# One-hot look-ups of a top-k selection: fp32 on VectorE and GpSimd, or bf16 on VectorE alone

## The chip, the cores and the metric

The kernel runs on one core of a Trainium2 chip. The core has five instruction streams: PE (TensorE, matrix products; its weight loads are listed apart as PEld), DVE (VectorE), ACT (ScalarE), POOL (GpSimd) and SP (SyncE, which here issues most DMA transfers). Each runs its own instructions in order and waits on semaphores for the others. Tiles lie in SBUF, results of PE in PSUM banks. The metric is device microseconds (us) of one execution.

## The reference

One step of a hybrid layer for 128 sample tokens (8 sequences of 16) and 256 prompt tokens: an RWKV-7 branch and a sparse-attention branch, mixed and added to x, then a PEER layer (a mixture over 16384 single-neuron experts), `x = x + gate2 * PEER(h2)`. The change lies in PEER's choice of experts. For each token and each of 8 heads a query of 128 numbers is cut into two halves. Each half is scored against 128 keys, and the 16 best keys of each half are kept, with their scores and indices. Their 256 sums are candidates, of which the 16 best are kept. Position p in the sorted candidates belongs to position p1 in the first list and p2 in the second; the expert is `i1[p1] * 128 + i2[p2]`. The look-ups are the two steps i1[p1] and i2[p2]: for each token, head and half, 16 positions (0 to 15) are replaced by the key indices (0 to 127) that stand there. The 16 sums go through a softmax to give the experts' weights; the layer's output is the sum over the experts of weight times gelu(h2 . u_e) times v_e.

## The kernel before

Tokens lie on the 128 partitions, in three groups: i = 0 is the sample group, i = 1 and 2 are the prompt. The branches and the mixing take the time up to about 840 us. Then come the query products and scores, the selection, and the experts. For the prompt all 16384 experts are computed densely, in 128 blocks of 128 (`dense_u` for h2 . u with a gelu, `weights` for the matrix of weights per token and expert, `dense_v` for the products with v). For the sample group the chosen experts' rows are gathered (`peer_sparse`): per pick, POOL issues an indirect DMA (line 1518), DVE multiplies the row of u by h2 and sums (line 1529), ACT takes the gelu of four such sums (line 1532, tile `dots`), and DVE adds dots times the row of v into `acc` (line 1539). Heads are gathered in two halves, so `peer_select` is called four times: for i = 0 with four heads, twice, then for i = 1 and i = 2 with eight heads. The gathers run on beside everything that follows.

In `peer_select` (lines 1255 to 1341) DVE finds each list's 16 best by max, max_index and match_replace (lines 1273 to 1277), casts the indices to fp32 (`sif`, line 1279, tag `psf`), POOL adds the candidates (line 1284), DVE finds the best 16 of them (lines 1293 to 1297), and from their places in the candidate list works out the positions in the two sorted lists (`jf`, tag `pjf`, lines 1299 to 1309, with `st`, tag `pst`, as an aid). The look-ups follow, in blocks of one half and four heads, so 2 + 2 + 4 + 4 = 12 blocks. A block is a tile of 128 partitions x 4 heads x 16 picks x 16 places: DVE compares each pick's position with 0 to 15 (line 1315, a one-hot), POOL multiplies by the key indices (line 1317), DVE sums over the 16 places (line 1318). The tile's tag `poh` has two buffers, so the third block can begin only when the sum of the first is done; the same tag held a transposed h2 before.

Behind the look-ups come the softmax (Exp on ACT, line 1322), and for i = 0 the row numbers for the gathers, for i = 1 and 2 three transposes whose result `weights` needs.

The order of the instructions on each engine isn't written by hand: the tile framework orders them by a simulated timeline, so that the selection is interleaved with `dense_u`, the gathers and the beginning of `weights`. Tags and their numbers of buffers set who must wait for whom. The fp32 weights of most dense blocks are cut into a high and a low part (line 227 on ACT, line 231 on DVE or POOL), and some 36 blocks are multiplied whole. `G` (line 1445, ACT) is the gelu that empties the PSUM bank of a `dense_u` block (tag `fx`).

Of the kernel before, what the change touches and what calls it, by code (L numbers as in the profile page):

```python
# [14 lines left out]
BF16 = mybir.dt.bfloat16  # L15
I32 = mybir.dt.int32
U32 = mybir.dt.uint32
AF = mybir.ActivationFunctionType
OP = mybir.AluOpType
AX = mybir.AxisListType  # L20
# [172 lines left out]
class K:  # L193
# [1034 lines left out]
    def scores_head(self):  # L1228
        nc = self.nc
        self.h2f = self.t([128, 8, 256], tag="h2f", pool=self.qpool)  # L1230
        self.keysT = self.t([128, 8, 128], tag="keysT", pool=self.qpool)
        nc.sync.dma_start(self.keysT, self.I["keysT"])
        self.qp = self.t([128, 8, NT], tag="qp", pool=self.qpool)

    def scores_s(self, u):

        nc = self.nc
        W = self.wload(self.I["w_pq"][:, u], 256)
        q = self.t([128, 256], tag="pq")
        nc.scalar.activation(q, self.natp(W, 256, self.h2T, 0), AF.Copy)  # L1240
        p = self.ps([128, 2, 128], tag="cp")
        for c in range(2):
            nc.tensor.transpose(p[:, c], q[:, c * 128:(c + 1) * 128], self.ident)
        nc.scalar.activation(self.qp[:, 2 * u:2 * u + 2, 0:128], p, AF.Copy)
# [10 lines left out]
    def peer_select(self, i, h0=0, nh=8):  # L1255

        nc = self.nc
# [4 lines left out]
        for hb in range(0, nh, 4):  # L1262
            for half in range(2):
                pr = slice(64 * half, 64 * half + 64)
                p = self.ps([128, 4, 128], tag="dx")
# [4 lines left out]
                for c in range(4):  # L1270
                    h = hb + c
# [6 lines left out]
        sif = self.t([128, 2, 8, 16], tag="psf")[:, :, :nh]  # L1278
# [21 lines left out]
        jf = self.t([128, 2, 8, 16], tag="pjf")[:, :, :nh]  # L1300
# [7 lines left out]
        nc.vector.scalar_tensor_tensor(st, j1, 64.0, st, op0=OP.add, op1=OP.min)  # L1308
        nc.vector.tensor_tensor(j2, j2, st, op=OP.subtract)
        idx = self.t([128, 2, 8, 16], tag="pix", bufs=2)[:, :, :nh]  # L1310
        for half in range(2):
            for h in range(0, nh, 4):
                hs = slice(h, h + 4)
                oh = self.t([128, 4, 16, 16], tag="poh", bufs=2)
                nc.vector.tensor_tensor(oh, jf[:, half, hs].unsqueeze(3).to_broadcast([128, 4, 16, 16]),
                                        self.c["io16"].unsqueeze(1).unsqueeze(1).to_broadcast([128, 4, 16, 16]), op=OP.is_equal)
                nc.gpsimd.tensor_tensor(oh, oh, sif[:, half, hs].unsqueeze(2).to_broadcast([128, 4, 16, 16]), op=OP.mult)
                nc.vector.tensor_reduce(out=idx[:, half, hs], in_=oh, op=OP.add, axis=AX.X)

        gw = self.t([128, nh, 16], tag=f"pg{i}{h0}", pool=self.pool if i else self.hpool2)  # L1320
        nc.vector.tensor_tensor(gw, fv, fv[:, :, 0:1].to_broadcast([128, nh, 16]), op=OP.subtract)
# [13 lines left out]
        p = self.ps([128, 3, 128], tag="dx")  # L1335
# [362 lines left out]
```

## Time and profile before

| | us |
|---|---|
| runs | 1856.91, 1863.67, 1869.19 (median 1863.67) |
| profiled execution | 1860.99, span 1859.2 |
| look-ups, first start to last | 917.1 to 1097.8 |
| busy, PE / DVE / ACT / POOL | 1740.9 / 1379.4 / 693.3 / 724.1 |

A row of a line reads: line, engine, operation, result <- inputs by tile names, how many, then least/median/longest ns. In rows that group a stretch, "x" counts instructions and the figures stand in microseconds. "DMA share" is the mean busy share of the 16 DMA engines; PEclk is the granted clock of TensorE, 1.00 being full. A wait is written as who waited (engine, tile, line) <- for whom, with its total, its number and its longest.

### The profile page before, as it was taken

How to read it: one execution, taken by the hardware profiler on the slowest of the kernel's cores; microseconds unless marked ns; L12 is line 12 of the kernel's file. 1: busy time of each engine (PE TensorE's matmuls, PEld its weight loads, DVE VectorE, ACT ScalarE, POOL GpSimd, SP SyncE). 2: the span in 40 equal slices, each digit the busy share in tenths (PEclk: the TensorE clock that was granted, in tenths of full speed). 3: DMA queues.
4: the chain of work that ended last, by engine and by line, in shares of the span. 5: the costliest groups of instructions: out<-in, count | busy, mean ns of one | idle time of the engine just before them, and what ended most of it. 6: DMA issues, size and time to landing. Idle time of an engine off the chain costs nothing. (4 is left out here: it accounts for less than half of the span.)

```text
span 1859.2 us, 33617 instructions
## 1 busy us (share of the span) xinstructions
PE 1740.9 (94%) x12621; PEld 1436.3 (77%) x12621; DVE 1379.4 (74%) x2905; ACT 693.3 (37%) x1402; POOL 724.1 (39%) x763
## 2 busy tenths in 40 slices
PE   7997999999999989899988979999999888999998
PEld 4985888877877867798877869999975556776765
DVE  4549678767767745445999999899967777787773
ACT  4432333333243333334221135478842222333332
POOL 2331333223223210024255566563346676465541
PEclk8996999999999989899998989999999999999999
DMA  8421563454264274655487969975489999999994
GB/s 307 141 79 34 168 224 91 147 168 137 78 218 137 70 243 151 213 174 179 148 313 284 359 244 331 383 291 182 164 294 369 375 374 356 351 373 344 347 344 157
DMA packets 181083, 434.11 MB, mean 233 GB/s; under 512 B 39348, under 2 KB 78388, under 8 KB 180920
## 3 DMA queue, kind: packets, MB, share of 16 engines
q1 hardware_dynamic: 144056, 297.73, 46.8%
q0 software_dynamic: 36864, 134.23, 19.3%
q8 instruction: 99, 1.62, 0.3%
q14 instruction: 64, 0.52, 0.1%
HBM read 401.65 MB, written 30.24 MB: 232 GB/s over the span
## 5 line engine op out<-in xcount | busy, mean ns | idle before, releaser
L231 DVE TENSOR_TENSOR wl<-w,wh 128x1024 fp32r<-128x1024 f32 x278 | 351.2, 1269 | 138.5 <-PE mm L223 64.3
L227 ACT ACTIVATE wh<-w 128x1024 fp32r<-128x1024 f32 x282 | 295.3, 1053 | 221.6 <-PE mm L223 88.0
L223 PE MATMUL fx<-h2h,wl 128*128 128x256 f32 x736 | 214.3, 291 | 10.4 <-DVE wl L231 10.3
L1518 POOL DMA_INDIRECT raw<-in_pu,pe x128 | 161.9, 1265 | 154.5 <-DVE acc L1539 46.6
L223 PE MATMUL fx<-h2h,wh 128*128 128x256 f32 x736 | 215.6, 293 | 4.3 <-ACT wh L227 3.2
L1518 POOL DMA_INDIRECT raw<-in_pv,pe x128 | 169.8, 1327 | 121.0 <-PE dx L223 45.4
L223 PE MATMUL fx<-h2l,wh 128*128 128x256 f32 x736 | 209.8, 285 | 0.0
L1539 DVE SCALAR_TENSOR_TENSOR acc<-raw,dots,acc 128x1024 f32<-128x1024 f32 x127 | 169.8, 1337 | 17.9 <-DMA raw<-in_pv,pe 16.7
L1529 DVE SCALAR_TENSOR_TENSOR raw<-raw,sh 128x1024 f32<-128x1024 f32 x128 | 163.4, 1291 | 17.1 <-DMA raw<-in_pu,pe 16.7
L223 PEld LDWEIGHTS fx<-h2h,wl 128*128 128x128 f32 x736 | 140.1, 190 | 14.4 <-DVE wl L231 12.7
L223 PEld LDWEIGHTS fx<-h2h,wh 128*128 128x128 f32 x736 | 140.9, 191 | 10.1 <-ACT wh L227 4.5
L223 PE MATMUL fx<-h2f,w 128*128 128x256 f32 x576 | 133.5, 394 | 14.4 <-ACT G L1445 14.4
L223 PEld LDWEIGHTS fx<-h2l,wh 128*128 128x128 f32 x736 | 140.4, 191 | 2.1 <-issue 1.7
L223 PEld LDWEIGHTS fx<-h2f,w 128*128 128x128 f32 x576 | 112.9, 198 | 33.3 <-ACT G L1445 16.4
L223 PE MATMUL mm<-LTh,wh 128*128 128x384 f32 (+1 forms) x344 | 121.9, 355 | 1.7 <-ACT wh L227 1.0
L223 PE MATMUL mm<-LTl,wh 128*128 128x384 f32 (+1 forms) x344 | 120.7, 351 | 1.2 <-POOL LTl L477 1.2
L223 PE MATMUL mm<-LTh,wl 128*128 128x384 f32 (+1 forms) x344 | 121.0, 352 | 0.0
L223 PE MATMUL mm<-wh,LTh 128*128 128x256 f32 (+1 forms) x360 | 105.4, 293 | 0.6 <-ACT qx L876 0.6
L223 PE MATMUL mm<-wh,LTl 128*128 128x256 f32 (+1 forms) x360 | 104.6, 291 | 0.0
L223 PE MATMUL mm<-wl,LTh 128*128 128x256 f32 (+1 forms) x360 | 104.4, 290 | 0.0
L1367 POOL TENSOR_TENSOR G<-G,wg 128x144 f32<-128x144 f32 (+1 forms) x64 | 61.7, 988 | 85.6 <-ACT wg L1364 85.5
L223 PEld LDWEIGHTS mm<-wh,LTh 128*128 128x128 f32 x360 | 70.1, 195 | 4.6 <-issue 2.7
(549 smaller groups left out, 4193.3 us busy)
## 6 DMA issues: line engine op xcount, KB each, us to landing
w<-in_puT SPq DMA_DIRECT2D x128, 512.0 KB, 6.1
w<-in_pv SPq DMA_DIRECT2D x128, 512.0 KB, 6.8
w<-in_w_in SPq DMA_DIRECT2D x70, 512.0 KB, 4.5
w<-in_w_ada SPq DMA_DIRECT2D x48, 512.0 KB, 4.2
cKT<-in_cKT SPq DMA_DIRECT2D x32, 256.0 KB, 4.2
cV<-in_cV SPq DMA_DIRECT2D x32, 256.0 KB, 4.5
w<-in_w_pq SPq DMA_DIRECT2D x16, 512.0 KB, 3.6
d<-wst SPq DMA_DIRECT2D x8, 832.0 KB, 4.3
```

The lines of the kernel that those rows point to most:

```text
L223: return self.nc.tensor.matmul(out, l, r, start=start, stop=stop, skip_group_check=True, **kw)
L227: self.nc.scalar.activation(hi, src, AF.Copy)
L231: (self.nc.vector if eng == "v" else self.nc.gpsimd).tensor_tensor(lo, src, hi, op=OP.subtract)
L1367: (nc.vector if w is p else nc.gpsimd).tensor_tensor(g, g, w[:, :, c0:c1], op=OP.mult)
L1518: d = nc.gpsimd.indirect_dma_start(out=u, out_offset=None, in_=src, in_offset=bass.IndirectOffsetOnAxis(ap=e[:, j:j + 1], axis=0))
L1529: nc.vector.scalar_tensor_tensor(u, u, 1.0, h2, op0=OP.mult, op1=OP.mult, accum_out=dots[:, j:j + 1])
L1539: nc.vector.scalar_tensor_tensor(acc, v, dots[:, j:j + 1], acc, op0=OP.mult, op1=OP.add)
```

## The change

A constant `ioe` is made once: the numbers 0 to 15 in bf16, each repeated 16 times, so that its inner dimension runs over 16 equal values. In each call the positions are copied to bf16 (`jb`). A block's tile `o2` holds two bf16 halves in the same number of bytes as the fp32 tile before: the one-hot and the spread indices. ACT copies the key indices into the second half, spread over the picks. DVE compares `jb` with `ioe`; the order of the dimensions is now head, place, pick, so that picks are innermost. DVE multiplies the halves, in bf16, and sums over the places, which now lie 16 elements (32 bytes) apart. All numbers are whole and below 256, which bf16 holds exactly. POOL's twelve multiplications are gone.

```diff
@@ scores_head
         self.qp = self.t([128, 8, NT], tag="qp", pool=self.qpool)
+        self.ioe = self.t([128, 16, 16], BF16, tag="ioe", pool=self.qpool)
+        nc.vector.tensor_copy(self.ioe, self.c["io16"].unsqueeze(2).to_broadcast([128, 16, 16]))
@@ peer_select
         idx = self.t([128, 2, 8, 16], tag="pix", bufs=2)[:, :, :nh]
+        jb = self.t([128, 2, 8, 16], BF16, tag="pjb")[:, :, :nh]
+        nc.vector.tensor_copy(jb, jf)
         for half in range(2):
             for h in range(0, nh, 4):
                 hs = slice(h, h + 4)
-                oh = self.t([128, 4, 16, 16], tag="poh", bufs=2)
-                nc.vector.tensor_tensor(oh, jf[:, half, hs].unsqueeze(3).to_broadcast([128, 4, 16, 16]),
-                                        self.c["io16"].unsqueeze(1).unsqueeze(1).to_broadcast([128, 4, 16, 16]), op=OP.is_equal)
-                nc.gpsimd.tensor_tensor(oh, oh, sif[:, half, hs].unsqueeze(2).to_broadcast([128, 4, 16, 16]), op=OP.mult)
-                nc.vector.tensor_reduce(out=idx[:, half, hs], in_=oh, op=OP.add, axis=AX.X)
+                o2 = self.t([128, 2, 4, 16, 16], BF16, tag="poh", bufs=2)
+                nc.scalar.activation(o2[:, 1], sif[:, half, hs].unsqueeze(3).to_broadcast([128, 4, 16, 16]), AF.Copy)
+                oh, sx = o2[:, 0], o2[:, 1]
+                nc.vector.tensor_tensor(oh, jb[:, half, hs].unsqueeze(2).to_broadcast([128, 4, 16, 16]),
+                                        self.ioe.unsqueeze(1).to_broadcast([128, 4, 16, 16]), op=OP.is_equal)
+                nc.vector.tensor_tensor(oh, oh, sx, op=OP.mult)
+                nc.vector.tensor_reduce(out=idx[:, half, hs], in_=oh.rearrange("p h c k -> p h k c"), op=OP.add, axis=AX.X)
```

In the kernel after, line 1319 is the copy on ACT, 1321 the comparison, 1323 the multiplication, 1324 the sum, 1314 the copy of the positions; other lines of `peer_select` up to there stand 2 further down, lines behind it 6.

The order on the engines moves with the edit. First DVE, at the first two blocks of i = 1 (`pjf` and `pjb` are the positions, `pix` the result, `acc` and `raw` the gathered experts). Before:

```order
L1306 TENSOR_SCALAR pst_11001<-pjf_10997 128x128
L1315 TENSOR_TENSOR poh_11007<-pjf_10997,clate 128x1024
L1315 TENSOR_TENSOR poh_11011<-pjf_10997,clate 128x1024
L1539 SCALAR_TENSOR_TENSOR acc_11650<-raw_12293,dots_12147,acc_11650 128x1024
L1307 SCALAR_TENSOR_TENSOR pst_11001<-pjf_10997,pst_11001 128x128
L1539 SCALAR_TENSOR_TENSOR acc_11650<-raw_12360,dots_12147,acc_11650 128x1024
L1318 TENSOR_REDUCE pix_11006<-poh_11007 128x64
L1308 SCALAR_TENSOR_TENSOR pst_11001<-pjf_10997,pst_11001 128x128
L1539 SCALAR_TENSOR_TENSOR acc_11650<-raw_12363,dots_12147,acc_11650 128x1024
L1318 TENSOR_REDUCE pix_11006<-poh_11011 128x64
```

After, at the same blocks:

```order
L1314 CAST pjb_11017<-pjf_11007 128x256
L1539 TENSOR_TENSOR dots_12169<-dots_12169,pg_2022_10501 128x4
L1321 TENSOR_TENSOR poh_11019<-pjb_11017,ioe_9835 128x1024
L1321 TENSOR_TENSOR poh_11024<-pjb_11017,ioe_9835 128x1024
L1545 SCALAR_TENSOR_TENSOR acc_11672<-raw_12312,dots_12169,acc_11672 128x1024
L1323 TENSOR_TENSOR poh_11019<-poh_11019 128x1024
L1323 TENSOR_TENSOR poh_11024<-poh_11024 128x1024
L1545 SCALAR_TENSOR_TENSOR acc_11672<-raw_12315,dots_12169,acc_11672 128x1024
L1324 TENSOR_REDUCE pix_11016<-poh_11019 128x64
L1324 TENSOR_REDUCE pix_11016<-poh_11024 128x64
```

The two multiplications stand on DVE now, between comparison and sum, and the arithmetic on `pst` is all done before the first comparison, since `jb` is copied for both halves at once.

On POOL, at the first blocks of i = 0 (`pcd` are the candidates). Before:

```order
L1284 TENSOR_TENSOR pcd_10658<-psv_10592 128x4x56
L1284 TENSOR_TENSOR pcd_10658<-psv_10592 128x4x8
L1317 TENSOR_TENSOR poh_10487<-poh_10487,psf_10444 128x1024
L1284 TENSOR_TENSOR pcd_10658<-psv_10592 128x4x16
L1317 TENSOR_TENSOR poh_10491<-poh_10491,psf_10444 128x1024
L1518 DMA raw_11652<-in_pu,pe_2023_10504 128x1024
```

After:

```order
L1286 TENSOR_TENSOR pcd_10664<-psv_10598 128x4x56
L1286 TENSOR_TENSOR pcd_10664<-psv_10598 128x4x8
L1286 TENSOR_TENSOR pcd_10664<-psv_10598 128x4x16
L1524 DMA raw_11674<-in_pu,pe_2025_10510 128x1024
L1524 DMA raw_11677<-in_pu,pe_2025_10510 128x1024
```

The multiplications are gone, and the candidates and the gathers follow one another.

On ACT, at the third and fourth block of i = 1. Before:

```order
L1445 ACTIVATE G_11261<-fx_11434 128x256
L1445 ACTIVATE G_11261<-fx_11446 128x256
L1445 ACTIVATE G_11261<-fx_11458 128x256
L1445 ACTIVATE G_11261<-fx_11470 128x256
L1269 ACTIVATE psc_11043<-dx_11038 128x512
```

After:

```order
L1538 ACTIVATE dots_12169<-dots_12169 128x4
L1451 ACTIVATE G_11283<-fx_11468 128x256
L1319 ACTIVATE poh_11029<-psf_10950 128x1024
L1451 ACTIVATE G_11283<-fx_11480 128x256
L1319 ACTIVATE poh_11034<-psf_10950 128x1024
L1451 ACTIVATE G_11283<-fx_11492 128x256
```

The copies of the spread indices stand between the gelus of the dense experts; each of these two waits for the sum of the block whose buffer it takes.

## The prediction

> **What bounds the kernel now.** I read the page first, for the span and for which engine is fullest over the whole.
>
> ```profile
> span 1859.2 us, 33617 instructions
> PE 1740.9 (94%) x12621; PEld 1436.3 (77%) x12621; DVE 1379.4 (74%) x2905; ACT 693.3 (37%) x1402; POOL 724.1 (39%) x763
> ```
>
> PE is busy 94% of the span, so the look-ups can shorten the kernel only where PE stands idle. The edited lines run between 917 and 1098 us (the rows of the look-ups below give their first and last start), so the second view is the table of stretches, cut at those times and at the changes of work behind them.
>
> ```profile
> core 0: us, PE busy (x) PEld busy (x) DVE busy (x) ACT busy (x) POOL busy (x), PEclk, DMA share, GB/s
> 917.00:1100.00 183.00, 156.71 (x716) 132.84 (x714) 182.42 (x587) 35.47 (x73) 100.98 (x78) 0.93 0.79 286
> 1100.00:1400.00 300.00, 294.19 (x2294) 280.12 (x2295) 267.88 (x372) 192.34 (x419) 148.75 (x125) 1.00 0.76 277
> 1400.00:1600.00 200.00, 177.20 (x625) 117.26 (x624) 152.74 (x192) 52.60 (x83) 126.03 (x105) 0.95 0.99 371
> 1600.00:1859.20 259.20, 247.83 (x1131) 182.83 (x1129) 183.72 (x224) 88.77 (x135) 117.46 (x90) 0.99 0.86 316
> ```
>
> In the stretch of the selection DVE is busy 182.42 of 183.00 us, and PE only 156.71: 26.3 us of PE time are lost here, more than in any other of these rows but the DMA-bound one and nearly as much as there (22.8 and 11.4 us in the last two, 5.8 us in the second). DVE sets the pace of the selection, and an average of 74% hides it. Behind it, from 1100 to 1400 us, PE is busy 98%; from 1400 to 1600 us the DMA engines are at 0.99.
>
> The third view is the waits in that stretch (who waited for whom, total, times, longest).
>
> ```profile
> ACT G L1445 <- PE fx L223: 65.4, 21, 6.2
> ACT dots L1532 <- DVE raw L1529: 42.8, 7, 10.0
> PE fx L223 <- ACT G L1445: 14.4, 5, 5.7
> POOL poh L1317 <- DVE poh L1315: 8.6, 5, 4.5
> ```
>
> The chain is DVE first: ACT waits 42.8 us for the gathered dot products (line 1529) before their gelu (line 1532); the gelus of the dense experts (G, line 1445) queue behind that on ACT; and PE waits 14.4 us for those to free its PSUM banks. So whatever DVE saves here should be felt by PE, and what holds ACT is felt by PE too.
>
> **The change part by part.** These are the rows of the look-ups (least/median/longest ns of one, then first and last start).
>
> ```profile
> L1315 DVE TENSOR_TENSOR poh<-pjf,clate x12: 1206/1214/1270, 917.1 to 1085.5; 128x1024 f32<-128x1024 f32 x12
> L1317 POOL TENSOR_TENSOR poh<-poh,psf x12: 2352/3189/3349, 918.4 to 1088.8; 128x1024 f32<-128x1024 f32 x12
> L1318 DVE TENSOR_REDUCE pix<-poh x12: 1193/1207/1216, 923.0 to 1097.8; 128x64 f32<-128x1024 f32 x12
> L1307 DVE SCALAR_TENSOR_TENSOR pst<-pjf,pst x4: 2124/2312/2434, 918.6 to 1073.6; 128x64 f32<-128x64 f32 x2, 128x128 f32<-128x128 f32 x2
> L1308 DVE SCALAR_TENSOR_TENSOR pst<-pjf,pst x4: 197/240/281, 921.3 to 1079.3; 128x64 f32<-128x64 f32 x2, 128x128 f32<-128x128 f32 x2
> ```
>
> Lines 1307 and 1308 do the same operation on the same shapes, and one takes 2312 ns where the other takes 240. The timeline (start, duration) shows why; after the first pair stand the six other long DVE instructions of the stretch, and the usual durations of their lines in it.
>
> ```profile
> 918.39 2.35 POOL L1317 TENSOR_TENSOR poh<-poh,psf 128x1024 f32<-128x1024 f32 x1 [4.48 <-DVE poh L1315]
> 918.62 2.19 DVE L1307 SCALAR_TENSOR_TENSOR pst<-pjf,pst 128x64 f32<-128x64 f32 x1
> ...
> 960.78 2.85 DVE L1529 SCALAR_TENSOR_TENSOR raw<-raw,sh 128x1024 f32<-128x1024 f32 x1
> 995.32 3.37 DVE L1539 SCALAR_TENSOR_TENSOR acc<-raw,dots,acc 128x1024 f32<-128x1024 f32 x1
> 1009.50 3.36 DVE L1529 SCALAR_TENSOR_TENSOR raw<-raw,sh 128x1024 f32<-128x1024 f32 x1
> 1075.99 3.37 DVE L1529 SCALAR_TENSOR_TENSOR raw<-raw,sh 128x1024 f32<-128x1024 f32 x1
> 1086.59 3.36 DVE L231 TENSOR_TENSOR wl<-w,wh 128x1024 fp32r<-128x1024 f32 x1
> 1089.87 3.39 DVE L1539 SCALAR_TENSOR_TENSOR acc<-raw,dots,acc 128x1024 f32<-128x1024 f32 x1
> ```
>
> ```profile
> L1529 DVE SCALAR_TENSOR_TENSOR raw<-raw,sh x28: 1186/1208/3372, 940.8 to 1082.0; 128x1024 f32<-128x1024 f32 x28
> L1539 DVE SCALAR_TENSOR_TENSOR acc<-raw,dots,acc x26: 1258/1271/3393, 953.3 to 1098.9; 128x1024 f32<-128x1024 f32 x26
> L231 DVE TENSOR_TENSOR wl<-w,wh x3: 1209/1215/3362, 1086.6 to 1096.6; 128x1024 fp32r<-128x1024 f32 x3
> ```
>
> The POOL multiplication that starts at 918.39 ends at 920.74, and the DVE instruction that starts beside it ends at 920.81: a DVE instruction with two inputs in SBUF stands until POOL's is done. The "busy" of DVE contains this standing. *Removed: the hold-ups.* Line 1307: 4 x (2.31 - 0.24) = 8.3 us. The six others: 19.70 us in sum, less 3 x 1.208 + 2 x 1.271 + 1.215 = 7.38, gives 12.3. Together -20.6 us of DVE. I take it whole, because no POOL operation of that kind takes the place of the 12; the gathers' POOL instructions stay as they were, and the three additions for the candidates (line 1284) too.
>
> For the rest these rows give prices; the last three are of the view that groups by line and shape (us in all, then mean ns of one).
>
> ```profile
> L1354 DVE TENSOR_TENSOR oh<-wA,wB x64: 670/683/1142, 1115.3 to 1357.8; 128x512 f32<-128x512 f32 x64
> L1279 DVE CAST psf<-psi x4: 203/258/367, 904.0 to 1053.4; 128x128 f32<-128x128 uint32 x2, 128x256 f32<-128x256 uint32 x2
> L1301 DVE CAST pjf<-pja x4: 214/410/1625, 915.0 to 1068.7; 128x128 f32<-128x128 uint32 x2, 128x256 f32<-128x256 uint32 x2
> L227 ACT ACTIVATE wh<-w x5: 1043/1043/1057, 1083.6 to 1094.2; 128x1024 fp32r<-128x1024 f32 x5
> ```
>
> ```profile
> L684 DVE TENSOR_TENSOR TX<-TL,NL 48x225 f32<-48x225 f32 x8 | 4.8, 604 | 0.1
> L687 DVE COPY TX<-TL 48x256 f32<-48x256 f32 x8 | 3.2, 406 | 0.2
> L686 DVE TENSOR_REDUCE TL<-TX 48x15 f32<-48x225 f32 x8 | 3.0, 376 | 0.2
> ```
>
> *Comparison, now bf16.* Same 1024 columns, half the bytes. No row of before has a two-input instruction with only bf16; the bounds are the fp32 row, 1.214 us (no gain), and the time of half as many fp32 elements, 0.683 us (line 1354). I take the lower, because both operands now run along 16 adjacent elements of two bytes: 12 x (0.683 - 1.214) = -6.4 us (to 0). [...]
>
> *Multiplication, moved to DVE.* 12 more instructions, +8.2 us at 0.683 (to +14.6 at 1.214).
>
> *Reduction, now over a stride.* It sums bf16 elements 32 bytes apart. Its time now is 1.207 us for 1024 elements; with the 0.376 us of the 225-element reduction (line 686) that is (1207 - 376) / 799 = 1.04 ns per element and 0.142 us fixed. Line 687 reads one input transposed, with a step of 16 words: on that line 256 elements would take 0.408 us, and it takes 0.406, so no surcharge. Line 684 reads two inputs with such a step: 604 ns, where 225 elements on that line take 376, so 1.01 ns per element more. The change has one strided input; the nearest row is 687, whose surcharge is nil, and I take a little above it, +2 us for the 12. The bounds are 0 and 12 x 1024 x 1.01 ns = +12.4 us.
>
> *The bf16 copy of the positions* (line 1314 of after): 4 casts of 128 or 256 columns by line 1279, 4 x 0.26 = +1.1 us; line 1301 was once held to 1.6 us, so up to +6.5. The constant `ioe` is one more such cast, +0.3 us, in the mixing stage where PE is the busy one; there it costs nothing, and 0.3 us without that cover.
>
> *Spread indices, on ACT.* 12 copies of 128x1024 by line 227, 12 x 1.043 = 12.5 us, on an engine busy 35.47 of 183 us. Their input is ready with the cast of line 1279, long before the positions; but eight of the twelve also need a `poh` buffer, which the reduction of two blocks earlier frees. While ACT stands there, its queue behind it (qp, the score copies, G) stands, and PE for their banks; and DVE's multiplication needs the copy. Bounds: 0, and the 14.4 us that PE stands behind ACT today a second time; I take +2 us.
>
> The sum on DVE: -20.6 - 6.4 + 8.2 + 2 + 1.1 + 2 = -13.7 us. What is late next is PE, with 26.3 - 13.7 = 12.6 us of idle left, so the stretch can shrink by that much. From 1100 to 1400 us PE is 98% busy and its work only starts sooner, so the gain passes through. For the part behind it, 200 of 759 us are at a DMA share of 0.99; I take that quarter of the gain as lost and keep three quarters, -10 us. Against the profiled execution's own 1860.99 us (1.8 us around the span) that is 1851; the median of the runs, 1863.67, stands 2.7 us above that execution.
>
> **The rivals.**
>
> *The strided reduction pays.* For it: line 684. Against it: line 687. Price: halfway, since one of two inputs is strided, 12 x 1024 x 0.5 ns = +6.2 in place of +2, so -9.5 on DVE and -7 at the end: 1854. At the whole surcharge -3.3, so -2.5 at the end: 1858. [...]
>
> *Everything carries.* No surcharge, no ACT wait, no loss behind: -20.6 - 6.4 + 8.2 + 1.1 = -17.7, so 1843. For it: DVE's 99.7%, PE's idle of 26.3 us. Against it: the DMA share of 0.99.
>
> *The gain is swallowed.* PE reaches the DMA-bound stretch earlier and waits there: 1861. For it: 0.99 and 371 GB/s. Against it: the share is 0.76 and 0.79 before, so transfers have room to move forward.
>
> *ACT's queue blocks (slower).* Each of the eight copies that need a freed buffer stands for as long as PE's waits behind ACT last today, 14.4 / 5 = 2.9 us, and DVE and PE stand with it: 8 x 2.9 = 23 us in place of my 2, against -15.7 for the rest, +7; with the three quarters for what gains and losses carry, 1866, and at the longest such wait, 8 x 5.7 = 46, up to 1884. It decides from a mean wait of 15.7 / 8 = 2.0 us. For it: ACT executes in order, and DVE's backlog makes it wait up to 10.0 us today. Against it: the copies are small beside 81% idle time.
>
> *bf16 brings nothing (slower, or the change doesn't do what it says).* Both two-input instructions at 1.214 and the whole stride: -20.6 + 14.6 + 12.4 + 1.1 + 2 = +9.5, so 1868. [...] Against it: the adjacent inner runs.
>
> **How the numbers follow.** Forecast 1851: 0.33. Strided reduction 1854 to 1858: 0.20. Everything carries, 1843: 0.18. Swallowed, 1861: 0.12. ACT blocks, 1866 to 1884: 0.10. bf16 brings nothing, 1868: 0.07. The range from 1837 to 1872 takes in all of these but the worse half of the ACT case, and at the low end leaves some 6 us, about the distance between two runs of before, for the order of the other work, which changes with the edit. A measurement can tell 1% of 1863.67, 18.6 us: faster means below 1845, slower above 1882. Faster: most of "everything carries" and the lower edge of the forecast, 0.25. Slower: the tail of the ACT case and some of the unpriced reordering, 0.07. Within 1%: 0.68.
>
> **What would show it.** Right: no DVE instruction of 2 us or more in the look-ups; line 1307 (1309 of after) at 0.24 us; comparison and multiplication near 0.68, reduction near 1.2; POOL busy some 38 us less in the stretch (12 x 3.189); the selection's end earlier by 10 to 15 us with DVE still above 95%. Wrong: the reduction at 1.7 us or more; comparison at 1.2; ACT waiting for the reduction (line 1324 of after) by 2 us or more at a time; or the selection shorter and the stretch with the DMA at 0.99 longer by the same.

## The result and the profile after

| kernel | median us | runs | ratio to before (95%) |
|---|---|---|---|
| before | 1861.96 | 11 | |
| after | 1851.03 | 11 | 0.9942 (0.9920 to 0.9965) |

The change makes the kernel 10.9 us faster, 0.6%, and the interval excludes no change. The profiled execution of after has a span of 1850.2 us. Its look-ups, from the view of single lines (least/median/longest ns, first and last start):

```profile
L1309 DVE SCALAR_TENSOR_TENSOR pst<-pjf,pst x4: 200/278/293, 920.1 to 1069.8; 128x64 f32<-128x64 f32 x2, 128x128 f32<-128x128 f32 x2
L1314 DVE CAST pjb<-pjf x4: 219/284/357, 923.0 to 1070.8; 128x128 bf16<-128x128 f32 x2, 128x256 bf16<-128x256 f32 x2
L1319 ACT ACTIVATE poh<-psf x12: 1039/1056/1057, 906.9 to 1079.8; 128x1024 bf16<-128x1024 f32 x12
L1321 DVE TENSOR_TENSOR poh<-pjb,ioe x12: 680/688/754, 924.2 to 1082.5; 128x1024 bf16<-128x1024 bf16 x12
L1323 DVE TENSOR_TENSOR poh<-poh x12: 683/686/751, 927.4 to 1083.8; 128x1024 bf16<-128x1024 bf16 x12
L1324 DVE TENSOR_REDUCE pix<-poh x12: 1982/2002/2134, 930.2 to 1088.7; 128x64 f32<-128x1024 bf16 x12
```

The 2.3 us of line 1307 (here 1309) have become 0.28; comparison and product take 0.69 each; and the sum over the 32-byte step takes 2.00 us where 1.21 stood. From the table of stretches, the selection counted from the first cast of the key indices (line 1279, here 1281) to the end of the last sum. Before:

```profile
core 0: us, PE busy (x) PEld busy (x) DVE busy (x) ACT busy (x) POOL busy (x), PEclk, DMA share, GB/s
904.00:1099.00 195.00, 169.27 (x776) 143.11 (x774) 194.42 (x685) 36.65 (x75) 101.91 (x80) 0.93 0.76 275
```

After:

```profile
906.70:1090.70 184.00, 165.58 (x776) 141.63 (x774) 182.19 (x698) 44.78 (x84) 73.45 (x67) 0.96 0.81 289
```

The selection is 11.0 us shorter, with DVE still busy 99%; 776 products of PE lie in either. POOL's busy time has fallen by 28 us and not by the 38 that the prediction names as a sign: its 12 products had taken 34.7 us in all (2.91 us in the mean, where 12 times the median was reckoned), and its other work in the stretch took 6 us more. ACT's has risen by 8. One instruction of DVE that isn't part of the look-ups still stands, a gathered dot product of 2.22 us beside an addition of candidates on POOL (line 1286). What follows takes as long as before: from the start of the selection's last act, the copy of the second transposed result on ACT (line 1339, after 1345), to the end of the span.

```profile
L1339 ACT ACTIVATE pT<-dx x2: 491/491/491, 1021.0 to 1099.5; 128x384 f32<-128x384 f32 x2
```

```profile
L1345 ACT ACTIVATE pT<-dx x2: 490/490/490, 1014.2 to 1091.3; 128x384 f32<-128x384 f32 x2
```

1859.2 - 1099.5 = 759.7 us before, 1850.2 - 1091.3 = 758.9 after. This difference is called "the rest" below. Single executions reach the selection at different times: its first cast starts between 903.5 and 913.3 us in the profiles of this document, and line 1023, some 750 us earlier, already between 152.0 and 160.5. The start of the last `pT` moves with that. So the experiments are read by the rest and by the length of the selection, from its first cast to the last `pT`: 195.5 us before and 184.6 after.

### The profile page after: what moved, and what is told of

Its sections match the earlier page's. It is cut to its first block, busy times and chain, and to the rows that moved or that the text cites. A ratio compares the mean times of both kernels' runs of the same rounds, so it can differ in the third digit from the quotient of the medians.

```text
span 1850.2 us, 33639 instructions
## 1 busy us (share of the span) xinstructions
PE 1736.5 (94%) x12621; PEld 1434.4 (78%) x12621; DVE 1372.4 (74%) x2922; ACT 702.0 (38%) x1412; POOL 684.7 (37%) x751
## 5 line engine op out<-in xcount | busy, mean ns | idle before, releaser
L1524 POOL DMA_INDIRECT raw<-in_pu,pe x128 | 163.1, 1274 | 178.3 <-DVE acc L1545 42.5
L1373 POOL TENSOR_TENSOR G<-G,wg 128x144 f32<-128x144 f32 (+1 forms) x64 | 55.7, 894 | 88.7 <-ACT wg L1370 88.7
L223 PEld LDWEIGHTS mm<-LTh,wh 128*128 128x128 f32 (+1 forms) x344 | 66.6, 194 | 10.1 <-issue 3.6
```

The source lines that it names most:

```text
L223: return self.nc.tensor.matmul(out, l, r, start=start, stop=stop, skip_group_check=True, **kw)
L1373: (nc.vector if w is p else nc.gpsimd).tensor_tensor(g, g, w[:, :, c0:c1], op=OP.mult)
L1524: d = nc.gpsimd.indirect_dma_start(out=u, out_offset=None, in_=src, in_offset=bass.IndirectOffsetOnAxis(ap=e[:, j:j + 1], axis=0))
```

## The experiments

The theory: DVE's time in the selection sets when the selection ends, and that moment goes to the end of the kernel one to one; the change took the hold-ups by POOL away and gave a good part of it back in the strided sum. The rivals: a quarter or all of a gain is lost in the DMA-bound stretch; the hold-ups cost nothing at the end; ACT's queue takes a part. All medians, ratios to before with 95% intervals, and from each profile the starts of the first cast and of the last `pT`, the time between them, and the rest. Each ratio is taken against executions of before that were run beside that kernel, with medians from 1860.66 to 1863.29 us, so a difference of medians of two rows holds up to 2.6 us of that:

| kernel | median us | ratio | first cast | last pT | selection | rest |
|---|---|---|---|---|---|---|
| before | 1861.96 | | 904.0 | 1099.5 | 195.5 | 759.7 |
| after | 1851.03 | 0.9942 (0.9920 to 0.9965) | 906.7 | 1091.3 | 184.6 | 758.9 |
| e1_tree | 1843.18 | 0.9899 (0.9871 to 0.9927) | 908.6 | 1081.4 | 172.8 | 762.9 |
| e2_fp32_dve | 1872.78 | 1.0063 (1.0042 to 1.0084) | 903.5 | 1106.0 | 202.5 | 763.6 |
| g_fp32 | 1860.27 | 0.9985 (0.9969 to 1.0002) | 911.3 | 1102.6 | 191.3 | 759.7 |
| e3_twice | 1896.34 | 1.0179 (1.0148 to 1.0211) | 913.3 | 1136.3 | 223.0 | 759.4 |
| g_twice | 1881.68 | 1.0119 (1.0090 to 1.0148) | 909.3 | 1123.8 | 214.5 | 755.4 |
| e4_bf16_pool | 1857.11 | 0.9981 (0.9958 to 1.0004) | 906.8 | 1095.8 | 189.0 | 756.4 |
| e6_bufs4 | 1857.14 | 0.9967 (0.9944 to 0.9990) | 908.0 | 1093.4 | 185.4 | 762.7 |
| t_gate40 | 1846.83 | 0.9915 (0.9884 to 0.9946) | 910.8 | 1066.4 | 155.6 | 777.7 |
| t_wide | 1843.05 | 0.9913 (0.9883 to 0.9942) | 905.5 | 1070.5 | 165.0 | 767.1 |

### e1_tree: no strided sum

```diff
-                nc.vector.tensor_reduce(out=idx[:, half, hs], in_=oh.rearrange("p h c k -> p h k c"), op=OP.add, axis=AX.X)
+                for m in (8, 4, 2):
+                    nc.vector.tensor_tensor(oh[:, :, :m], oh[:, :, :m], oh[:, :, m:2 * m], op=OP.add)
+                nc.vector.tensor_tensor(idx[:, half, hs], oh[:, :, 0], oh[:, :, 1], op=OP.add)
```

> Kernel after, with the strided reduction (12 x 2.002 us) replaced by four bf16 additions that halve the places (512, 256, 128 and 64 results), all over adjacent picks. By the 0.688 us of a bf16 product of 1024 columns and the 0.25 us of small two-input instructions the four take about 0.42 + 0.28 + 0.22 + 0.24 = 1.16 us, so DVE gets back 12 x 0.84 = 10 us. Theory 'DVE's time in the selection goes to the end one to one': 1841 us. Rival 'a quarter is lost in the DMA-bound stretch': 1843.5. Rival 'DVE's time there does not end the kernel, the gain came from POOL's relief or from the order': 1851.

Measured 1843.18 us. The additions, by line:

```profile
L1325 DVE TENSOR_TENSOR poh<-poh x36: 210/280/475, 932.2 to 1076.9; 128x512 bf16<-128x512 bf16 x12, 128x256 bf16<-128x256 bf16 x12, 128x128 bf16<-128x128 bf16 x12
L1326 DVE TENSOR_TENSOR pix<-poh x12: 201/217/230, 937.0 to 1078.3; 128x64 f32<-128x64 bf16 x12
```

Their durations come to 11.1 + 2.6 us for the 12 blocks, 1.14 us per block in place of 2.00. The ends of short instructions overlap with what follows; counted from each start to DVE's next start it is 0.81 us per block, where the strided sum has 1.92. The selection is 11.8 us shorter than in after, and the median falls by 7.9. So DVE's time in the selection does carry to the end; between one to one (1841) and three quarters (1843.5) this run doesn't decide. Part of it stops at PE: DVE ends its last sum 12.3 us earlier than in after (at 1078.5 and 1090.8 us), but the transposes of that sum then stand behind other products in PE's queue, and the last `pT` starts 9.9 us earlier. e1_tree is clearly faster than before; against after the two intervals overlap.

### e2_fp32_dve and g_fp32: the hold-ups alone

The kernel before, with one word changed:

```diff
-                nc.gpsimd.tensor_tensor(oh, oh, sif[:, half, hs].unsqueeze(2).to_broadcast([128, 4, 16, 16]), op=OP.mult)
+                nc.vector.tensor_tensor(oh, oh, sif[:, half, hs].unsqueeze(2).to_broadcast([128, 4, 16, 16]), op=OP.mult)
```

> Kernel before, with the fp32 multiplication on VectorE in place of GpSimd and nothing else. Theory 'the hold-ups of DVE by POOL cost 20.6 us': -20.6 + 12 x 1.214 = -6 us, 1856 if all of it carries, 1857.5 at three quarters; no DVE instruction with two inputs over 2 us is left. Rival 'the hold-ups hid behind something': +14.6 us, 1876. Rival 'bf16 alone made the gain': slower than before by some us.

Measured 1872.78 us, 11.5 us slower than before on the same chip, not 6 faster. As far as the time goes, the theory failed here. The hold-ups are gone in the profile all the same:

```profile
L1307 DVE SCALAR_TENSOR_TENSOR pst<-pjf,pst x4: 204/249/291, 918.2 to 1085.0; 128x64 f32<-128x64 f32 x2, 128x128 f32<-128x128 f32 x2
L1317 DVE TENSOR_TENSOR poh<-poh,psf x12: 1205/1220/1226, 918.3 to 1099.4; 128x1024 f32<-128x1024 f32 x12
```

So something else was added. The view that groups DVE's lines, from the selection's first cast to the last `pT`, shows it (count, busy us, mean ns, idle time before and what ended it). Before:

```profile
L1529 DVE SCALAR_TENSOR_TENSOR raw<-raw,sh 128x1024 f32<-128x1024 f32 x28 | 40.1, 1434 | 0.0
L1539 DVE SCALAR_TENSOR_TENSOR acc<-raw,dots,acc 128x1024 f32<-128x1024 f32 x26 | 37.5, 1442 | 0.3 <-DMA raw<-in_pv,pe 0.3
L231 DVE TENSOR_TENSOR wl<-w,wh 128x1024 fp32r<-128x1024 f32 x3 | 5.8, 1929 | 0.0
```

e2_fp32_dve:

```profile
L1529 DVE SCALAR_TENSOR_TENSOR raw<-raw,sh 128x1024 f32<-128x1024 f32 x34 | 41.2, 1214 | 2.2 <-DMA raw<-in_pu,pe 2.2
L1539 DVE SCALAR_TENSOR_TENSOR acc<-raw,dots,acc 128x1024 f32<-128x1024 f32 x29 | 37.1, 1280 | 0.2 <-DMA raw<-in_pv,pe 0.2
L231 DVE TENSOR_TENSOR wl<-w,wh 128x1024 fp32r<-128x1024 f32 x5 | 6.1, 1214 | 0.0
```

The scheduler orders by its own timeline; with a longer stretch of DVE work planned there it placed 6 more gathered dot products, 3 more sums and 2 more weight splits ahead of the selection's end: 6 x 1.21 + 3 x 1.28 + 2 x 1.21 = 13.5 us of DVE. With the product's 12 x 1.22 = 14.6 us and without the 20.6 us of hold-ups that makes +7.5, and the selection is 7.0 us longer. The work that was moved ahead did not shorten the rest (763.6 us for 759.7). In its first 300 us DVE is busy 252 us where before has 268, but PE is busy 98% there in both. Why the rest is 3.9 us longer isn't settled. To test the account of the order, the gathers from the 55th on were made to wait for the last `pT`, which gives DVE nearly the gathered rows of before (28 dot products and 25 sums; `tdone` names that copy):

```diff
+            self.ng += 1
+            pace = self.pace or (self.tdone if self.ng > 54 else None)
-            if self.pace is not None:
-                self.tc.add_manual_dep(d.ins, self.pace, ...
+            if pace is not None:
+                self.tc.add_manual_dep(d.ins, pace, ...
```

> The fp32 multiplication on VectorE as in e2_fp32_dve, and the gathers from the 55th on wait for the selection's last transposed result, so that DVE has as many gathered rows to work on before the selection's end as the kernel before (28 dot products, 25 sums; e2 had 33 and 29). Theory 'e2 lost what the scheduler pulled in, and the hold-ups are worth their 20.6 us': -20.6 + 14.4 for the moved products + 2.4 for two more weight splits, -4, so about 1857. Rival 'the hold-ups are worth nothing at the end': it stays at 1873.

Measured 1860.27 us, and before 1863.29 beside it: 12.5 us less than e2 (by the two ratios 14.5), where the limit keeps back 6 dot products and 4 sums, 12.4 us; the 2 splits stay ahead. The ratio's interval just includes no change, so that this version gains anything isn't shown. But DVE does 12 x 1.22 = 14.6 us more look-up work in it than before, at no loss: that much at least came back at the end. The selections give the size: 191.3 us against 195.5, with 14.6 us more for the product, 2.4 for 2 splits and one sum less (1.3), leave 4.2 + 14.6 + 2.4 - 1.3 = 19.9 us for the hold-ups; e2 in the same way 14.6 + 13.5 - 7.0 = 21.1. The limit in the kernel before, without the changed word, was not run.

### e3_twice and g_twice: how much of a delay reaches the end

In e3 the line of the strided sum stands twice; g_twice has the same limit on the gathers besides.

> Kernel after, with each of the 12 strided reductions done twice: 12 x 2.002 = 24 us more of DVE in the selection, nothing else. Theory 'one to one': 1875 us. Rival 'three quarters': 1869. Rival 'swallowed or slack': 1851 to 1855.

> The doubled reduction of e3_twice with the same limit on the gathers (28 and 25 instead of 32 and 28; after has 28 and 24). Theory 'the selection's length goes to the end one to one, and e3 lost 45 us because the longer selection also pulled gathers in': 1851 + 24 + some 4 for three more splits = 1879. Rival 'a delay of DVE costs the end nearly twice its length by itself': stays near 1896.

Measured 1896.34 and 1881.68 us. Without the limit, 24 us of DVE cost 45.3 us; no theory had expected more than 24. Here too the order had drawn gathers in. e3_twice, the same view:

```profile
L1536 DVE SCALAR_TENSOR_TENSOR raw<-raw,sh 128x1024 f32<-128x1024 f32 x33 | 40.0, 1214 | 6.0 <-DMA raw<-in_pu,pe 6.0
L1546 DVE SCALAR_TENSOR_TENSOR acc<-raw,dots,acc 128x1024 f32<-128x1024 f32 x28 | 35.6, 1270 | 0.0
L231 DVE TENSOR_TENSOR wl<-w,wh 128x1024 fp32r<-128x1024 f32 x5 | 6.0, 1209 | 0.0
```

After has 28, 24 and 3 of these, so 5 dot products, 4 sums and 2 splits came ahead. By durations that is 24 + 5 x 1.21 + 4 x 1.27 + 2 x 1.21 = 37.6 us; counted from start to next start, as for e1_tree, 22.6 + 4.6 + 4.5 + 2.2 = 33.9. With 4.4 us more of DVE idle, mostly waiting for rows, the second count comes to 38.3, and the selection is 38.4 us longer. The other 6.9 us of the 45.3 are not the selection's: in this profile its first cast starts 6.6 us later than in after's, and why isn't settled. With the limit:

```profile
L1538 DVE SCALAR_TENSOR_TENSOR raw<-raw,sh 128x1024 f32<-128x1024 f32 x28 | 34.1, 1219 | 4.0 <-DMA raw<-in_pu,pe 3.9
L1548 DVE SCALAR_TENSOR_TENSOR acc<-raw,dots,acc 128x1024 f32<-128x1024 f32 x25 | 31.9, 1275 | 1.3 <-DMA raw<-in_pv,pe 1.1
L231 DVE TENSOR_TENSOR wl<-w,wh 128x1024 fp32r<-128x1024 f32 x5 | 6.0, 1208 | 0.0
```

24 + 1.3 + 2.4 us of work and some 4 of waiting are 32 by durations; the selection is 29.9 us longer and the median 30.7. The rest is 759.4 and 755.4 us, both inside the 755.4 to 762.9 us of the kernels that do 28 gathered dot products in the selection. A delay goes to the end one to one: three quarters of 29.9 would be 22, and the ratios of after and g_twice, from end to end of their intervals, leave 23 to 42 us.

### e4_bf16_pool: the product back on GpSimd, in bf16

```diff
-                nc.vector.tensor_tensor(oh, oh, sx, op=OP.mult)
+                nc.gpsimd.tensor_tensor(oh, oh, sx, op=OP.mult)
```

> Kernel after, with the bf16 multiplication back on GpSimd. DVE gives away 12 x 0.686 = 8.2 us and gets hold-ups: if POOL takes 3.2 us for bf16 too and holds DVE ten times in twelve as before, +20.6, so 1851 + 12.4 = 1863; if POOL takes half as long in bf16, +10, so 1853. If the hold-ups are not what counts, 1843.

Measured 1857.11 us, between the two; the interval includes no change from before. POOL takes 2.28 us in the median where the fp32 product took 3.19, and the hold-ups are back, on two comparisons, two sums of gathered rows and one small multiplication:

```profile
L1323 POOL TENSOR_TENSOR poh<-poh x12: 2117/2282/3106, 925.2 to 1088.9; 128x1024 bf16<-128x1024 bf16 x12
```

```profile
L1321 DVE TENSOR_TENSOR poh<-pjb,ioe x12: 668/684/2605, 924.4 to 1085.4; 128x1024 bf16<-128x1024 bf16 x12
L1545 DVE SCALAR_TENSOR_TENSOR acc<-raw,dots,acc x24: 1257/1267/5606, 958.4 to 1095.4; 128x1024 f32<-128x1024 f32 x24
L1539 DVE TENSOR_TENSOR dots<-dots,pg x7: 135/140/4142, 952.7 to 1091.0; 128x4 f32<-128x4 f32 x7
```

The median of the comparison is the same 0.68 us, the longest 2.6. The 4.14 us on 128x4 elements start 0.1 us behind two products on POOL, which take 4.20. Against after the median is 6.1 us longer and the selection 4.4, with intervals that just overlap. That speaks for the product's leaving POOL as a part of the gain, though DVE pays 8.2 us for doing it itself.

### e6_bufs4: ACT's queue

Both uses of the tag `poh` get four buffers.

> Kernel after with four poh buffers instead of two, so that ACT's copies of the spread indices seldom wait for a reduction (after has 15.5 us of such waits, six times). Theory 'ACT's queue costs nothing at the end, since DVE stood idle only 1.8 of 183 us': the waits go, the time stays at 1851 +- 4. Rival 'ACT's queue blocks': up to those 15.5 us come back, 1836 to 1845.

From the waits of after between 905 and 1095 us, those of the copies:

```profile
ACT poh L1319 <- DVE pix L1324: 15.5, 6, 5.6
ACT poh L1319 <- DVE psf L1281: 14.4, 3, 8.9
```

With four buffers the first is gone:

```profile
ACT poh L1319 <- DVE psf L1281: 13.5, 4, 6.3
```

Measured 1857.14 us, no faster than after: that the waits are gone won nothing. The median is 6.1 us above after's, but the two intervals overlap, and the selections are 185.4 and 184.6 us long. Whether the difference is real isn't settled.

### e5_strides: the price of a step, by itself

Probes on DVE in the mixing stage of after, three times each: sums of 1024 elements into 64 over different steps, and the copy of line 687 with an adjacent one beside it. The kernel's own time (1866.19 us) holds the probes.

> Kernel after with a row of probes on DVE in the mixing stage, three times each, to be read by their durations and not by the kernel's time: reductions of 1024 elements, fp32 and bf16, over adjacent elements, over a step of 4 bytes (bf16), 32 bytes (bf16 as in the change; fp32) and 64 bytes (fp32), and fp32 copies of 48x256, adjacent and transposed like line 687. [...] Rival 'it is bf16 that is slow': bf16 2.0 us even over adjacent elements, fp32 1.2 at any step.

```profile
L1244 DVE TENSOR_REDUCE prr<-prx x3: 1160/1199/1220, 769.5 to 804.5; 128x64 f32<-128x1024 f32 x3
L1245 DVE TENSOR_REDUCE prr<-pry x3: 1200/1212/1212, 773.1 to 806.7; 128x64 f32<-128x1024 bf16 x3
L1246 DVE TENSOR_REDUCE prr<-pry x3: 1207/1214/1222, 775.9 to 809.5; 128x64 f32<-128x1024 bf16 x3
L1247 DVE TENSOR_REDUCE prr<-pry x3: 2031/2124/2182, 779.7 to 811.1; 128x64 f32<-128x1024 bf16 x3
L1248 DVE TENSOR_REDUCE prr<-prx x3: 1901/1947/1972, 783.2 to 814.3; 128x64 f32<-128x1024 f32 x3
L1249 DVE TENSOR_REDUCE prr<-prx x3: 2112/2129/2170, 786.2 to 818.2; 128x64 f32<-128x1024 f32 x3
L1250 DVE COPY prz<-prx x3: 268/272/277, 770.6 to 785.1; 48x256 f32<-48x256 f32 x3
L1251 DVE COPY prz<-prx x3: 357/364/368, 774.2 to 788.2; 48x256 f32<-48x256 f32 x3
```

In order: fp32 adjacent 1.20 us; bf16 adjacent 1.21; bf16 over a step of 4 bytes 1.21; bf16 over 32 bytes 2.12, the step of the change; fp32 over 64 bytes 1.95; fp32 over 32 bytes 2.13. In the sums it is the step and not the type. The last two rows settle the sign that the prediction misread: the transposed copy takes 364 ns, an adjacent one 272, so line 687 did carry a surcharge, 0.36 ns per element.

### t_gate40 and t_wide: further than the tree

t_gate40 is e1_tree with the gathers from the 41st on waiting for the last `pT`.

> The tree of additions of e1_tree, with the gathers from the 41st on waiting for the selection's end (20 dot products and 19 sums before it instead of 28 and 23). Theory 'one to one': the selection gets 8 x 1.21 + 4 x 1.27 = 15 us shorter on DVE, of which PE's idle time there (12.6 us in e1's stretch) lets at most 12 through: 1831, if the gathers find room later. Rival 'the DMA-bound stretch takes them back': 12 rows of 0.5 MB at the 371 GB/s of that stretch are 17 us, 1843 to 1848.

Measured 1846.83 us, no faster than e1_tree. The selection does end 15.0 us earlier, but the rest grows by 14.8. Two stretches behind the last `pT` of e1_tree, and two of t_gate40, cut to begin with the selection's end and to end at the same time:

```profile
1082.00:1382.00 300.00, 291.42 (x2273) 277.96 (x2274) 267.01 (x368) 193.06 (x419) 141.42 (x123) 0.99 0.77 277
1382.00:1582.00 200.00, 177.12 (x629) 117.14 (x628) 153.46 (x192) 52.61 (x83) 128.51 (x106) 0.96 0.98 366
```

```profile
1067.00:1367.00 300.00, 286.84 (x2288) 277.40 (x2286) 275.07 (x376) 190.27 (x416) 149.23 (x134) 0.99 0.80 290
1367.00:1582.00 215.00, 195.94 (x708) 129.94 (x707) 174.26 (x216) 61.74 (x95) 142.37 (x114) 0.98 1.01 382
```

Both kernels do nearly equal work in the first 300 us after the selection (2273 and 2288 products). The second stretch of t_gate40 is 15 us longer and as full of DMA: 1.01 at 382 GB/s over 215 us, for 0.98 at 366 over 200. The rival of its expectation had named 17 us for this, 1843 to 1848. And the selection itself holds fewer of PE's products, 702 for e1_tree's 778, which had to be done later: PE's idle time in it fell only from 11.1 to 5.9 us while it became 17.2 us shorter. So the prediction's rival, that a gain is swallowed behind the selection, is real for gathers put off.

t_wide is e1_tree with blocks of all the heads of a call, 8 blocks instead of 12.

> The tree of additions of e1_tree in blocks of all the heads of a call (8 blocks of 4 or 8 heads instead of 12 of 4; copy, comparison, product and additions twice as wide for i = 1 and 2). By the 0.15 us that an instruction costs beside its elements: 4 blocks x 6 DVE instructions x 0.15 = 3.6 us less, so 1840 against 1843 of e1, if one to one. Rival: the wider copy on ACT (2 us) and the longer steps keep DVE waiting, 1843 to 1850.

Measured 1843.05 us, the same as e1_tree. Its selection is 7.8 us shorter and the rest 4.2 us longer; its profiled execution was one of its faster ones (a span of 1837.6 us). Most of the 7.8 us is work put off: 2 dot products, 2 sums and 1 split fewer lie ahead of the end, some 6.2 us, and 732 of PE's products for 778. What the wider blocks give by themselves isn't settled.

## Why the prediction was right, and where it was wrong

The forecast of 1851 us met the median of 1851.03, but with luck: its largest error, in the strided sum, was offset by smaller ones, and it was counted from the profiled execution (1860.99), 2.7 us below the median of before that it had. Its view of the bottleneck held: DVE was 99% busy, its hold-ups went, and the time followed. One reading was off without effect: the 26.3 us of PE time lost in the selection are more than in the DMA-bound row too (22.8).

*Hold-ups, -20.6 us.* Right in mechanism: no instruction of the look-ups stands at 2.3 us any more (line 1309 takes 0.293 us at the longest). In before's profile all ten SCALAR_TENSOR_TENSOR and TENSOR_TENSOR instructions of DVE that began beside a product of line 1317 ended 0.08 to 1.09 us behind it; of those with one input, the sum of line 1318 from 1013.58 to 1014.77 us, beside a product from 1011.74 to 1015.07, took its usual 1.19 us, while the cast of line 1301 from 939.24 us stood beside an addition on POOL (line 1284, 939.79 to 940.77) and ended at 940.87. What decides which of them stand isn't shown, nor whether it matters that the inputs lie in SBUF. For the size, the selections of e2 and g_fp32 give 21.1 and 19.9 us; in g_fp32's time at least the 14.6 us that it spends elsewhere came back.

*Comparison and product.* 0.688 and 0.686 us were measured where 0.683 was taken: -6.3 and +8.2. The rival that bf16 brings nothing fell. The comparison went from 1.214 us to 0.688, and the product on DVE, which took 1.220 us in fp32 (e2), to 0.686; a sum over adjacent elements gained nothing by bf16 (1.212 against 1.199 us in the probes). Type and order of the dimensions changed together in comparison and product, so what each of them brings isn't shown; that the lower time needs adjacent elements, the reason given for taking it, was the author's estimate.

*The sum over a step, +2 us: this step failed.* It measured 12 x (2.002 - 1.207) = +9.5 us. The prediction compared a transposed copy (line 687) with a line drawn through reductions, found no surcharge, and gave this row more weight than line 684. An adjacent copy is faster than an adjacent reduction (0.272 us for 256 elements in the probes, where the line through reductions gives 0.408), and that difference hid the surcharge. Its rival "the strided reduction pays" had the mechanism and, between its 6.2 and 12.4, the size, though its times of 1854 to 1858 did not come. The probes bear out the surcharge for steps of 32 and 64 bytes (0.73 to 0.91 ns per element more). A step of 4 bytes cost nothing (1.214 against 1.212 us in bf16). No step between 4 and 32 bytes was tried, so where the surcharge begins isn't shown.

*Casts and ACT.* The four casts took 0.28 us each, where 0.26 was taken. The +2 us for ACT's waits were not there: DVE never stood idle before a multiplication, and e6 won nothing by more buffers. The rival "ACT's queue blocks" had its waits (15.5 us, up to 5.6 at a time) but not its effect; PE's waits behind the gelus are 11.1 us, where before had 14.4.

*The sum.* With these sizes it is -20.6 - 6.3 + 8.2 + 9.5 + 1.1 = -8.1 us on DVE and not -13.7. The scheduler also left 2 sums of gathered rows fewer ahead of the selection's end (24 for 26, 2.6 us), which gives -10.7; the selection became 10.9 us shorter. These 2.6 us are work put off, for which the prediction had no term. Whether they are a gain at the end isn't shown: in t_gate40 work put off was lost again, and the measured -10.9, with its interval from -14.9 to -6.5, takes in -8.1 as well.

*Three quarters.* For a delay this was wrong: g_twice carried its 29.9 us whole. For a gain the runs don't decide. After's -10.9 in the selection came as -10.9 in the time, e1_tree's further -11.8 as -7.9, and each interval takes in both shares. The reason given, the DMA share of 0.99 in a later stretch, did not show in after: the rest is as long as before (758.9 and 759.7 us). A limit does show further on, as less and less of PE's time is idle in the selection: 25.8 us before, 18.6 in after, 11.1 in e1_tree, 7.4 in t_wide, and t_wide is no faster than e1_tree. So -13.7 x 3/4 = -10 met the measured -10.9, where -10.7 on DVE and a share nearer one fit as well. The rival that all is swallowed fell, since the interval excludes no change; "everything carries" had the share of after but 9.6 us too much on DVE.

*What none of the rivals had:* that the order answers to the length of the look-ups. In e2 13.5 us of work, only moved, turned a saving of 6 us on DVE into a selection 7.0 us longer. The 6 us allowed in the range for "the order of the other work" were its only place, and too few.

## What to carry to other kernels

Where a scheduler sets the order, count the other instructions ahead of the point that sets the end, on before and after, ahead of reading a time as the price of an edit: a part undone may bring other work along, and a limit on that work makes the comparison cleaner. Price a strided access by a row with the same operation over adjacent elements beside it, never by the line of another operation. A forecast that meets the time says little on its terms: the sum and the share of it that carries have to be tested apart, for instance by doubling one known duration.

## What the runs showed of the hardware

A sum over elements 32 bytes apart took 2.1 us where adjacent ones took 1.2, the same for fp32 and bf16, and 4 bytes apart in bf16 cost nothing (1.21 us); four additions over adjacent bf16 do the same sum in 1.14 us by their durations.

Durations of short instructions in a row can mislead. In after's profile the 40 searches of line 1276 have a mean of 324 ns, against 283 for the same line (1274) before:

```profile
L1274 DVE FIND_INDEX8 psi<-psv,psc 128x8 uint32<-128x128 f32 x40 | 10.8, 283 | 0.0
```

```profile
L1276 DVE FIND_INDEX8 psi<-psv,psc 128x8 uint32<-128x128 f32 x40 | 11.7, 324 | 0.0
```

But from the start of such a search to the next start on DVE there are 202 ns on average in both (40 of each, worked out from the trace's starts): their ends overlap with what follows, and these searches became no slower.
